# A decoder layer on one core: buffers shared by hand over three stages, even token tiles first, a written order in gate/up, right-hand tiles on 64 bytes

## The chip, the core and the metric

The kernel runs on one core of a Trainium2 chip. The metric is the device time of one execution in microseconds (us); the kernel before has a median of 1450.23 us over three runs. The engines are TensorE (PE, with its weight loads as PEld), VectorE (DVE), ScalarE (ACT), GpSimd (POOL) and SyncE (SP), which issues the transfers (DMA). PE multiplies into PSUM, in banks of 512 float32 words per partition; the other operands lie in SBUF.

## The reference

One decoder layer in float32: 1024 tokens, model width 1024, feed-forward width 2816.

```python
h  = h + rmsnorm(concat(retention, attention) @ w_o, post_mix_norm)
hn = rmsnorm(h, pre_ffn_norm)
ff = (silu(hn @ w_gate) * (hn @ w_up)) @ w_down
h  = h + rmsnorm(ff, post_ffn_norm)
h  = h + rmsnorm(p @ w_ple_proj, ple_norm) * sigmoid(h @ w_ple_gate + b_ple_gate)
```

Ahead of the first line stand a combined input projection of the normalised tokens, retention in four heads and causal attention with latents in eight heads.

## The kernel before

**Arithmetic.** Each float32 operand is split into a high and a low part (`split`: an ACT copy that rounds, L81, and a subtract, L82, on DVE unless `sub` says otherwise). A product takes three matmuls, high by high, high by low, low by high (`products`, L94, or written out). The large multiplications of gate/up and down work on 2 x 2 blocks with seven products in place of eight. For that the operands are combined by sums and differences: on the token side T1 to T4 out of the blocks of an even and an odd token tile, on the weight side the `sums`.

**Stages and lines.** (1) Input projection and latents. (2) Retention, about 162 to 291 us. Inside its loop, `down_sums(q)` is called for the 11 quarters q of w_down: it loads the four blocks of `w_down[q]` in two transfers, makes four combinations on POOL (`combos`, L108 to L111) and stores them to `td[q]` in DRAM in three transfers; the down stage loads them from there. (3) Attention. (4) The projection by w_o, about 570 to 675 us. `project(t)` runs over the token tiles 0 to 7 in order. It loads `mt` (attention output, from DRAM `mo`), `mix` and `ht`, splits `mt`, does 24 matmuls into `po`, adds (L718), takes a Square with its sum on ACT into a scrap tile `junk`, scales (L722), adds the residual (L723), takes a second Square (L726), and scales again (L728) into `mix`. `rsqrt` (L117, L119) is one DVE and one POOL operation. `operands(t)` follows two tiles behind: for an even tile it transposes B11 and B21 into the operands `xh` and `xl`; for an odd tile it makes T1 to T4 on POOL (L108 to L111) from the odd tile and the even one ahead of it, and transposes those and B22. (5) Gate/up, about 690 to 1120 us. (6) Down, from about 1140 us: seven runs of `down` over the 11 quarters, in chunks of two, each chunk with one left-hand and one right-hand slot (`dslot`: a load into `draw`, of which there are five, and a split into `dring`, nine pairs). (7) The per-layer embedding gate (`pg`) and the output.

**Gate/up.** There are 22 matrices: w_gate and w_up in 11 quarters. Each has seven products, and a product is 12 matmuls (L813) of 128 x 128 by 128 x 512. All seven of one matrix write one PSUM tile `gu` of two 512-word halves, `bank[m][0]` and `bank[m][1]`, in turn:

```python
ORDER = ((B11, 0, 0, 0), (B21, 1, 0, 1), (T2, 0, 1, 0), (T1, 1, 1, 1), (T3, 0, 2, 0), (B22, 1, 3, 0), (T4, 0, 2, 1))
```

The columns are the token operand, the half of `gu`, the weight part and its place in the part. After each product its half is evicted: for n = 0, 2 and 3 by an ACT copy (L821), for n = 1, 4 and 5 by a DVE add onto such a copy (L826), which keeps accumulating in the half, for n = 6 directly. Evicted blocks go through `use` (L797 and beside it): Silu on ACT for w_gate, a multiplication on DVE for w_up, into `ga`. Two `gu` tiles exist at a time. `weight_part` splits one part of a matrix, three steps ahead of its product; `weight_sums` makes the combinations on POOL (L776 and beside it); `load` fetches a matrix of 1 MB. `down_operands(q)` combines `ga` on POOL into `dsums` and stores both to `ld[q]`.

`steps` lists the 154 products: (0, 0), (0, 1), (1, 0), (1, 1), the rest of matrix 0, the rest of matrix 1, and then matrix by matrix. The program text emits them in that order. The order in which each engine issues is another: the tile context is opened with a timeline planner, which takes ready instructions by its own cost estimate.

**Waits.** They are drawn from the emitted order by the tile that an instruction reads or writes. In the compiled program of before, the first matmul of a product in one half of `gu` carries a wait for the eviction of the product ahead of it in the other half, where both belong to one matrix.

**Addresses.** Pools lie on the left or the right side of SBUF. Every tile on the right begins 32 bytes past a multiple of 64; the left-hand tiles that PE reads begin on a multiple. `xh`, `xl` are on the left, the weight parts `gh`, `gl` on the right; in the down stage `draw` and `dring` are both on the right.

Of the kernel before, what the change touches and what calls it, by code (L numbers as in the profile page):

```python
# [20 lines left out]
P = 128  # L21
# [41 lines left out]
def hybrid_layer(ctx: ExitStack, tc: tile.TileContext, a: dict, out: bass.AP):  # L63
# [43 lines left out]
    def combos(t1, t2, t3, t4, b11, b12, b21, b22, eng):  # L107
        eng.tensor_tensor(out=t1, in0=b12, in1=b11, op=ALU.subtract)  # L108
        eng.tensor_tensor(out=t2, in0=b22, in1=t1, op=ALU.subtract)
        eng.tensor_tensor(out=t3, in0=b22, in1=b12, op=ALU.subtract)  # L110
        eng.tensor_tensor(out=t4, in0=b21, in1=t2, op=ALU.subtract)  # L111

# [12 lines left out]

    pack = const.tile([P, sum(PACK.values())], F32, name="pack")
# [21 lines left out]
    td = [dram.tile([4, P, 512], F32, name=f"td{q}") for q in range(NQ)]  # L148
# [258 lines left out]

    def down_sums(q):
        r1, r2, s = [raws.tile([P, S], F32, tag="raw", name=n) for n in ("wd1", "wd2", "wds")]
        sp.dma_start(out=r1, in_=a["w_down"][q][:, 0:2, :].rearrange("p i n -> p (i n)"))  # L410
        sp.dma_start(out=r2, in_=a["w_down"][q][:, 2:4, :].rearrange("p i n -> p (i n)"))
        c0, c1 = slice(0, 512), slice(512, S)
        combos(s[:, c0], s[:, c1], r1[:, c1], r2[:, c0], r1[:, c0], r1[:, c1], r2[:, c0], r2[:, c1], pool)
        sp.dma_start(out=td[q][0:2].rearrange("i p n -> p i n"), in_=s.rearrange("p (i n) -> p i n", i=2))
        sp.dma_start(out=td[q][2], in_=r1[:, c1])
        sp.dma_start(out=td[q][3], in_=r2[:, c0])

    down_q = 0
    g_ret = [1.0 - 2.0 ** (-5.0 - h) for h in range(RH)]
    pending = None  # L420
    for j in range(RH // 2):
# [14 lines left out]
        for hh in range(2):  # L436
# [9 lines left out]
            for hf in range(2):  # L446
# [236 lines left out]
    B11, B21, B22, T1, T2, T3, T4 = range(7)  # L683
    st_x = ExitStack()
    px = scoped(st_x, "px")
    xh, xl = [px.tile([P, 7, 4, HALF], F32R, name=n) for n in ("xh", "xl")]
    st3 = ExitStack()
    p3 = scoped(st3, "p3", 2)
    wpm = bcast(p3, a["w_post"], "wpm")
    wpf = bcast(p3, a["w_pref"], "wpf")  # L690
# [3 lines left out]
    def to_operand(i, j, src):  # L694
        nonlocal nblk
        pt = ps1("ptx", "tfto"[nblk % 4])
# [4 lines left out]
        split(xh[:, i, :, js], xl[:, i, :, js], pt.rearrange("p (k n) -> p k n", k=4))  # L701

    tiles = {}
    lo_, hi_ = slice(0, HALF), slice(HALF, D)

    def project(t):
        mt = p3.tile([P, 4, P], F32, name="mt")
        sp.dma_start(out=mt, in_=mo[t])
        mix, ht = [p3.tile([P, D], F32, name=n, bufs=4) for n in ("mix", "ht")]
        sp.dma_start(out=mix, in_=od[t])  # L710
        sp.dma_start(out=ht, in_=a["x"][t * P : (t + 1) * P])
        mh, ml = [p3.tile([P, 4, P], F32R, name=n) for n in ("mh", "ml")]
        split(mh, ml, mt)
# [6 lines left out]
        act.activation(p3.tile([P, D], BF16, name="junk", bufs=1), mix, AF.Square, accum_out=ss)  # L720
# [5 lines left out]
        act.activation(p3.tile([P, D], BF16, name="junk", bufs=1), ht, AF.Square, accum_out=ss)  # L726
        rsqrt(ss, ss, 1.0 / D)
        dve.scalar_tensor_tensor(out=mix, in0=ht, scalar=ss, in1=wpf, op0=ALU.mult, op1=ALU.mult)  # L728
        tiles[t] = (mix, ht)

    def operands(t):
        j = t // 2
        mix, ht = tiles[t]
        if t % 2 == 0:
            to_operand(B11, j, mix[:, lo_])
            to_operand(B21, j, mix[:, hi_])
        else:
            e, he = tiles[t - 1]
            combos(he[:, lo_], he[:, hi_], ht[:, lo_], ht[:, hi_], e[:, lo_], mix[:, lo_], e[:, hi_], mix[:, hi_], pool)
            to_operand(B22, j, mix[:, hi_])  # L740
            for i, src in ((T2, he[:, hi_]), (T1, he[:, lo_]), (T3, ht[:, lo_]), (T4, ht[:, hi_])):
                to_operand(i, j, src)

    for t in range(NT):
        project(t)
        if t >= 2:
            operands(t - 2)
    st_b.close()
    operands(NT - 2)
    operands(NT - 1)  # L750
    st3.close()
# [5 lines left out]
    graw = scoped(st_g, "graw", 2, side="right")  # L757
    gsl = scoped(st_g, "gsl", 4, side="right")
    gs = scoped(st_g, "gs", 3)
    gev = scoped(st_g, "gev", 1)  # L760
    gga = scoped(st_g, "gga", 2)

    mats = [(name, q) for q in range(NQ) for name in ("w_gate", "w_up")]
    raw, sums, parts, bank, part_sums, act_out = {}, {}, {}, {}, {}, {}

    def load(m):
        name, q = mats[m]
        raw[m] = graw.tile([P, 4, HALF], F32, tag="w", name=f"raw_{name}")
        sp.dma_start(out=raw[m], in_=a[name][q])

    def weight_sums(m):
        r = raw[m]
        s = sums[m] = gs.tile([P, 3, HALF], F32, tag="s", name="sums")
        pool.tensor_tensor(out=s[:, 1], in0=r[:, 2], in1=r[:, 3], op=ALU.add)
        pool.tensor_tensor(out=s[:, 0], in0=s[:, 1], in1=r[:, 0], op=ALU.subtract)
        pool.tensor_tensor(out=r[:, 2], in0=r[:, 0], in1=r[:, 2], op=ALU.subtract)  # L776
        pool.tensor_tensor(out=s[:, 2], in0=r[:, 1], in1=s[:, 0], op=ALU.subtract)

    def weight_part(m, p):
        src = (raw[m][:, 0:2], sums[m][:, 0:2] if p == 1 else None, raw[m][:, 2:4], sums[m][:, 2:3] if p == 3 else None)[p]  # L780
        n = src.shape[1]
        hi, lo = [gsl.tile([P, 2, HALF], F32R, tag=h, name=f"{h}_{mats[m][0]}")[:, :n] for h in ("gh", "gl")]
# [8 lines left out]
    def use(m, b, v):  # L791
        name, q = mats[m]
        dst = act_out[q][:, KEPT[b]]
# [5 lines left out]
    def product(m, n):  # L799
        name, q = mats[m]  # L800
        i, b, p, at = ORDER[n]
        if n == 0:
            pt = ps2("gu")
            bank[m] = pt[:, :HALF], pt[:, HALF:]
            if name == "w_gate":
                act_out[q] = gga.tile([P, 4, HALF], F32, name="ga")
        dst = bank[m][b]
        hi, lo = parts[m, p]
        x = 0
        for k in range(4):  # L810
            ks = slice(k * P, (k + 1) * P)
            for l, r in ((hi, xh), (hi, xl), (lo, xh)):
                pe.matmul(dst, l[:, at, ks], r[:, i, k, :], start=(n in (0, 1, 3) and x == 0), stop=(x == 11),  # L813
                          skip_group_check=True)
                x += 1

        s = part_sums.setdefault(m, {})
        if n in (0, 2, 3):
            nm = {0: "s1", 2: "u2", 3: "s5"}[n]
            s[nm] = gev.tile([P, HALF], F32, name=nm, bufs=(2 if n == 0 else 1))  # L820
# [3 lines left out]
        else:  # L824
            nm, blk = {1: ("s1", 0), 4: ("s5", 3), 5: ("u2", 1)}[n]
            dve.tensor_tensor(out=s[nm], in0=dst, in1=s[nm], op=ALU.add)  # L826
            use(m, blk, s[nm])

    def down_operands(q):
        ga = act_out[q]  # L830
        s = gs.tile([P, 3, HALF], F32, tag="s", name="dsums")
# [4 lines left out]
        sp.dma_start(out=ld[q][0:4].rearrange("i p n -> p i n"), in_=ga)  # L836
        sp.dma_start(out=ld[q][4:7].rearrange("i p n -> p i n"), in_=s)
# [7 lines left out]
    def when(i, rank, f, *args):  # L845
        todo[max(i, 0)].append((rank, f, args))

    for m in range(nmat):
        first = {0: at_step[m, 0], 1: at_step[m, 2], 2: at_step[m, 4], 3: at_step[m, 5]}
        for p, i in first.items():  # L850
            when(i - 3, 2, weight_part, m, p)
# [33 lines left out]
    def td_quad(i):  # L885
        return lambda q: td[q][i]
# [164 lines left out]
```

## Time and profile before

| what | value |
|---|---|
| median of three runs | 1450.23 us (1449.12 to 1450.68) |
| the profiled execution, its own time | 1453.09 us |
| its span, first to last instruction | 1451.3 us |
| PE busy | 1361.4 us, 94% of the span, 6732 matmuls and transposes |
| DVE / ACT / POOL busy | 767.4 (53%) / 538.5 (37%) / 427.2 us (29%) |
| mean granted clock of PE | 0.976 |
| DMA | 214.73 MB, 148 GB/s on the mean, queue 1 busy for 44.2% of 16 engines' span |
| largest line of the chain that ended last | PE `gu` L813, 30% of the span |

The profile is one execution, recorded by the hardware. Busy time is a sum over instructions, less their overlap; the granted clock is the share of full speed (2.4 GHz) that PE was given, 0.5 being the lower level of 1.2 GHz. Matmuls overlap in the pipeline: a row shows 0.40 us for one of 512 columns, while the next begins 0.23 us after it. A bracket behind a row gives the idle time of the engine ahead of it and the instruction whose end released it. The chain of waits follows the last instruction back, at each step to what released it.

### The profile page before, as it was taken

Reading aid. Unit: us, or ns where it says so; the run is one execution under the profiler, and the core shown is the slowest. Engines: PE = TensorE matmul, PEld = TensorE weight load, DVE = VectorE, ACT = ScalarE, POOL = GpSimd, SP = SyncE. Lnnn points to the kernel's source line nnn. Section 1 sums busy time; section 2 is a strip of 40 time slices with the busy share of each in tenths; the row PEclk is TensorE's granted clock in tenths of the full one; section 3 lists DMA queues with packets and bytes.
Section 4 is the critical chain, followed back from the end, with each engine's and each line's share of the span. In section 5 each row is a group of like instructions: output and inputs, shape, how many; then the busy total and the mean of one; then the engine's idle time right before and its main releaser. Section 6 shows DMA issues by size and latency. Waiting matters only on the chain.

```text
span 1451.3 us, 18194 instructions
## 1 busy us (share of the span) xinstructions
PE 1361.4 (94%) x6732; PEld 1134.0 (78%) x6732; DVE 767.4 (53%) x1198; ACT 538.5 (37%) x889; POOL 427.2 (29%) x333
## 2 busy tenths in 40 slices
PE   7999999999989998876899999999997999999998
PEld 6987988788768886655688888888885788888776
DVE  6456447526577675586344444434443554474653
ACT  5343221111565554344233333333332544444421
POOL 1100344400354243237144444444443000013300
PEclk9999999999999999986999999999999999999999
DMA  6137776812565641661123332232312966575422
GB/s 242 44 123 247 264 266 232 284 52 59 163 202 145 177 113 45 226 236 50 38 109 110 109 109 92 98 109 87 109 58 98 330 203 204 187 239 181 132 72 73
DMA packets 91320, 214.73 MB, mean 148 GB/s; under 512 B 9504, under 2 KB 24096, under 8 KB 88416
## 3 DMA queue, kind: packets, MB, share of 16 engines
q1 hardware_dynamic: 91232, 213.58, 44.2%
q8 instruction: 53, 0.87, 0.3%
q14 instruction: 35, 0.29, 0.1%
HBM read 144.86 MB, written 67.63 MB: 146 GB/s over the span
## 4 chain that ended last, share of the span: by engine, by line
PE 70%; DMA 8%; DVE 7%; issue 5%; POOL 5%; ACT 3%; SPq 1%; DVEq 0%; POOLq 0%; ACTq 0%
PE gu L813 30%; PE da L902 6%; PE pg L94 5%; PE fill L94 4%; PE pa L94 4%; PE db L902 3%; PE sc L94 3%; DMA wd<-in_w_down 2%; PE prg L94 2%; PE ptp L650 2%; PE prv L94 2%; PE pge L94 2%; PE pqk L94 1%; PE po L94 1%; DMA td<-wd 1%
## 5 line engine op out<-in xcount | busy, mean ns | idle before, releaser
L813 PE MATMUL gu<-xh,gh_w_gate 128*128 128x512 f32 x308 | 123.0, 399 | 5.1 <-ACT gh_w_gate L81 1.6
L813 PE MATMUL gu<-xh,gh_w_up 128*128 128x512 f32 x308 | 122.4, 398 | 2.3 <-DVE s L826 0.9
L813 PE MATMUL gu<-xh,gl_w_up 128*128 128x512 f32 x308 | 121.9, 396 | 1.6 <-DVE gl_w_up L82 1.6
L813 PE MATMUL gu<-xl,gh_w_gate 128*128 128x512 f32 x308 | 122.5, 398 | 0.0
L813 PE MATMUL gu<-xh,gl_w_gate 128*128 128x512 f32 x308 | 122.3, 397 | 0.0
L813 PE MATMUL gu<-xl,gh_w_up 128*128 128x512 f32 x308 | 122.0, 396 | 0.0
L119 POOL TENSOR_TENSOR s<-s,mhalf 128x1 f32<-128x1 f32 x32 | 28.6, 901 | 310.3 <-DVE s L117 310.2
L641 POOL TENSOR_TENSOR pr<-pr,ri 128x128 f32<-128x128 f32 (+3 forms) x64 | 73.8, 1164 | 109.3 <-DVE ri L640 97.3
L82 DVE TENSOR_TENSOR dl_r<-raw_r,dh_r 128x1024 fp32r<-128x1024 f32 (+1 forms) x42 | 47.7, 1135 | 81.9 <-ACT dh_r L81 70.4
L832 POOL TENSOR_TENSOR dsums<-ga 128x512 f32<-128x512 f32 x11 | 14.2, 1289 | 250.4 <-DVE ga L797 250.4
L826 DVE TENSOR_TENSOR s<-gu,s 128x512 f32<-128x512 f32 x44 | 30.4, 691 | 102.0 <-PE gu L813 102.0
L81 ACT CAST dh_r<-raw_r 128x1024 fp32r<-128x1024 f32 (+1 forms) x42 | 41.3, 982 | 105.9 <-PE da L902 52.4
L902 PE MATMUL db<-dh_r,dh_l 128*128 128x512 f32 x176 | 68.1, 397 | 8.3 <-ACT dh_r L81 8.3
L813 PEld LDWEIGHTS gu<-xh,gh_w_gate 128*128 128x128 f32 x308 | 58.3, 189 | 20.6 <-ACT gh_w_gate L81 2.0
L813 PEld LDWEIGHTS gu<-xh,gh_w_up 128*128 128x128 f32 x308 | 57.9, 188 | 17.8 <-DVE s L826 1.3
L813 PEld LDWEIGHTS gu<-xh,gl_w_up 128*128 128x128 f32 x308 | 57.9, 188 | 16.0 <-DVE gl_w_up L82 2.1
L902 PE MATMUL db<-dl_r,dh_l 128*128 128x512 f32 x176 | 69.3, 394 | 0.1
L813 PEld LDWEIGHTS gu<-xh,gl_w_gate 128*128 128x128 f32 x308 | 58.2, 189 | 14.3 <-DVE gl_w_gate L82 0.2
L902 PE MATMUL db<-dh_r,dl_l 128*128 128x512 f32 x176 | 69.3, 394 | 0.0
L813 PEld LDWEIGHTS gu<-xl,gh_w_gate 128*128 128x128 f32 x308 | 58.3, 189 | 14.0
L813 PEld LDWEIGHTS gu<-xl,gh_w_up 128*128 128x128 f32 x308 | 58.0, 188 | 13.9
L82 DVE TENSOR_TENSOR tl<-ptp,th 128x512 fp32r<-128x512 f32 (+1 forms) x80 | 49.7, 633 | 24.0 <-ACT th L81 22.8
(337 smaller groups left out, 3807.2 us busy)
## 6 DMA issues: line engine op xcount, KB each, us to landing
raw_l<-ld SPq DMA_DIRECT2D x77, 256.0 KB, 3.3
wd<-in_w_down SPq DMA_DIRECT2D x22, 512.0 KB, 4.7
raw_w_gate<-in_w_gate SPq DMA_DIRECT2D x11, 1024.0 KB, 4.8
raw_w_up<-in_w_up SPq DMA_DIRECT2D x11, 1024.0 KB, 4.8
ld<-ga SPq DMA_DIRECT2D x11, 1024.0 KB, 4.3
raw_r<-td SPq DMA_DIRECT2D x44, 256.0 KB, 4.0
ld<-dsums SPq DMA_DIRECT2D x11, 768.0 KB, 3.6
raw_r<-in_w_down SPq DMA_DIRECT2D x33, 256.0 KB, 4.6
```

Of the source, the lines that this page charges most:

```text
L81: act.copy(out=hi, in_=src)
L82: sub.tensor_tensor(out=lo, in0=src, in1=hi.bitcast(F32), op=ALU.subtract)
L94: pe.matmul(dst, l, r, start=(m == 0), stop=(m == n - 1))
L119: pool.tensor_tensor(out=dst, in0=dst, in1=mhalf[:, :n], op=ALU.pow)
L641: pool.tensor_tensor(out=pr_[:, :n], in0=pr_[:, :n], in1=ri.broadcast_to([P, n]), op=ALU.mult)
L650: pe.transpose(pt[:, m * P : (m + 1) * P], pb[qq][:, kk * P : (kk + 1) * P], ident)
L813: pe.matmul(dst, l[:, at, ks], r[:, i, k, :], start=(n in (0, 1, 3) and x == 0), stop=(x == 11), skip_group_check=True)
L826: dve.tensor_tensor(out=s[nm], in0=dst, in1=s[nm], op=ALU.add)
L832: pool.tensor_tensor(out=s[:, 1], in0=ga[:, 2], in1=ga[:, 3], op=ALU.add)
L902: pe.matmul(banks[j], l[:, ls], r[:, rs_], start=(fresh and q == 0 and m == 0), stop=(q == NQ - 1 and m == 2), skip_group_check=True)
```

## The change

Buffers. Right-hand tiles get a 32-byte pad ahead of them. From the projection to the end, most tiles that were drawn from pools become fixed views of five 8 KB `duo` tiles and a 12 KB `strip`: `blk[0..9]` are halves of `duo`s; they hold `mix` and `ht` in the projection, and the accumulators and two of the five `draw` buffers in the down stage. In gate/up the same `duo`s hold one of two raw weight buffers, `gga` (the old `ga`), the evicted parts, and `quad[4]`, which is at once `wd` (the w_down quarter) and, in its first three fourths, `gs[2]` (the old `dsums`). `mt` and `junk` of a tile share bytes, two sets in turn. `xh`/`xl` become 14 tiles, one per operand and part.

Projection. Tiles run in the order 0, 2, 4, 6, 1, 3, 5, 7. The split of `mt` subtracts on POOL. The second scaling (L728) becomes a DVE multiplication by `wpf` and an ACT copy with the scale. The combinations T1 to T4 are unchanged in number, in other buffers. The loads and splits for the first products stand ahead of `operands` of the last two tiles, the first two products between these, the next two behind them.

Gate/up. `product` and `evict` are split; `steps` is unchanged. From the fifth product on, everything is emitted inside `tc.manual_schedule()`, in which each engine issues as written. w_down's combinations (`wd_load`, `wd_sums`, `wd_store`) move here out of retention: per quarter one load of 1 MB, four POOL operations, one store of 1 MB.

Down. The first chunk's slots are emitted ahead of the last `down_sums` and `down_store`.

```diff
-    def combos(t1, t2, t3, t4, b11, b12, b21, b22, eng):
...
+    pad = ctx.enter_context(tc.tile_pool(name="pad", bufs=1, side="right"))
+    pad.tile([P, 8], F32, name="pad")
...
-    def down_sums(q):
-        r1, r2, s = [raws.tile([P, S], F32, tag="raw", name=n) for n in ("wd1", "wd2", "wds")]
...
-                for _ in range(1 + (hf and h > 0)):
-                    if down_q < NQ:
-                        down_sums(down_q)
-                        down_q += 1
...
+    duo = [pst.tile([P, 2 * D], F32, name=f"duo{i}") for i in range(5)]
+    blk = [duo[i][:, j * D : (j + 1) * D] for i, j in
+           ((3, 1), (0, 1), (2, 0), (3, 0), (0, 0), (1, 0), (2, 1), (4, 0), (4, 1), (1, 1))]
+    strip = pst.tile([P, 3 * D], F32, name="strip")
...
+    order = [0, 2, 4, 6, 1, 3, 5, 7]
+
+    def project(n):
+        t = order[n]
+        v = strip[:, 2 * D + n % 2 * HALF :][:, :HALF]
+        mt, junk = v.rearrange("p (k n) -> p k n", k=4), v.bitcast(BF16)
+        mh, ml = [pmo.tile([P, 4, P], F32R, name=n_) for n_ in ("mh", "ml")]
+        mix, ht = blk[n % 7], blk[7 + n % 3]
...
-        split(mh, ml, mt)
+        split(mh, ml, mt, sub=pool)
...
-        dve.scalar_tensor_tensor(out=mix, in0=ht, scalar=ss, in1=wpf, op0=ALU.mult, op1=ALU.mult)
+        dve.tensor_tensor(out=mix, in0=ht, in1=wpf, op=ALU.mult)
+        act.activation(mix, mix, AF.Copy, scale=ss)
...
+    graw = [pg_.tile([P, 4, HALF], F32, name="graw"), quad[0]]
+    gga = [quad[2], quad[3]]
+    gs = [v.rearrange("p (i n) -> p i n", i=3) for v in (strip[:, : 3 * HALF], strip[:, 3 * HALF :])] + [quad[4][:, :3]]
+    wd = quad[4]
...
+    def wd_load(q):
+        sp.dma_start(out=wd, in_=a["w_down"][q])
+
+    def wd_sums(q):
+        b11, b12, b21, b22 = [wd[:, i] for i in range(4)]
+        pool.tensor_tensor(out=b11, in0=b12, in1=b11, op=ALU.subtract)
...
+    def wd_store(q):
+        sp.dma_start(out=td[q], in_=wd)
...
+    load(0)
+    load(1)
+    weight_part(0, 0)
+    weight_part(1, 0)
+    operands(NT - 2)
+    for m, n in steps[:2]:
+        product(m, n)
+    operands(NT - 1)
+    for m, n in steps[2:4]:
+        product(m, n)
+    for m in range(2):
+        weight_sums(m)
+    for m, n in steps[:4]:
+        evict(m, n)
+    weight_part(0, 1)
+    weight_part(0, 2)
+
+    for q in range(NQ):
+        i = 14 * q
+        if q:
+            when(i + 1, down_sums, q - 1)
+        when(max(i + 2, 4), (lambda m: weight_sums(m)) if q else (lambda m: None), 2 * q + 1)
+        if q:
+            when(i + 3, down_store, q - 1)
+        when(i + 6, wd_load, q)
+        if q + 1 < NQ:
+            when(i + 9, weight_sums, 2 * q + 2)
+        when(i + 11, wd_sums, q)
+        when(i + 13, wd_store, q)
     for m in range(nmat):
+        for p, n in enumerate((0, 2, 4, 5)):
+            if m > 1 and p == 0 or m > 0 and p or p == 3:
+                when(max(at_step[m, n] - 3, 4), weight_part, m, p)
+        if m + 2 < nmat:
+            when(at_step[m, 4], load, m + 2)
+    with tc.manual_schedule():
+        for i, (m, n) in enumerate(steps):
+            if i < 4:
+                continue
+            for f, args in todo[i]:
+                f(*args)
+            product(m, n)
+            evict(m, n)
...
+    draw = [pd_.tile([P, D], F32, name=f"draw{i}") for i in range(3)][::-1] + blk[7:9]
+    acc = blk[:7] + blk[9:]
...
+    early_slots = [down_slots(0, wd_quad(0), 0)]
+    down_sums(NQ - 1)
+    down_store(NQ - 1)
```

`product` is as before up to its last matmul, and `evict(m, n)` is what followed there. `weight_sums` has its last two lines exchanged. The remaining edits rename views.

## Rows read from the trace of the kernel before

**Rows 1.** Windows: us, five engines' busy (x), granted clock, DMA share, GB/s.

```profile
162.00:291.00 129.00, 123.56 (x743) 108.41 (x742) 72.73 (x128) 21.97 (x32) 62.17 (x48) 0.99 0.76 261
...
639.00:676.50 37.50, 16.00 (x69) 11.40 (x67) 28.16 (x37) 16.58 (x30) 20.25 (x19) 0.56 0.42 154
...
710.00:1107.00 397.00, 397.00 (x1702) 319.63 (x1703) 167.10 (x181) 134.26 (x183) 169.31 (x116) 1.00 0.26 94
```

**Rows 2.** Timeline of PE, mid gate/up: start us, us, operation.

```profile
712.87 0.40 PE L813 MATMUL gu<-xh,gh_w_up 128*128 128x512 f32 x1
...
715.67 0.40 PE L813 MATMUL gu<-xh,gh_w_gate 128*128 128x512 f32 x1
```

**Rows 3.** Timeline, ends of gate/up; bracketed: idle before, releaser.

```profile
695.00 0.50 PE L813 MATMUL gu<-xh,gl_w_up 128*128 128x512 f32 x1 [1.62 <-DVE gl_w_up L82]
...
701.84 0.50 PE L813 MATMUL gu<-xh,gh_w_gate 128*128 128x512 f32 x1 [1.44 <-ACT s L821]
...
706.13 0.49 PE L813 MATMUL gu<-xh,gh_w_gate 128*128 128x512 f32 x1 [1.22 <-DVE s L826]
...
1104.87 0.40 PE L813 MATMUL gu<-xh,gh_w_up 128*128 128x512 f32 x1
...
1107.87 0.59 ACT L821 COPY s<-gu 128x512 f32<-128x512 f32 x1 [2.20 <-PE gu L813]
...
1108.51 0.50 PE L813 MATMUL gu<-xh,gh_w_up 128*128 128x512 f32 x1 [0.68 <-ACT s L821]
...
1112.43 0.49 PE L813 MATMUL gu<-xh,gh_w_up 128*128 128x512 f32 x1 [0.85 <-DVE s L826]
```

**Rows 4.** Chain of waits: start us, us, what, x instructions.

```profile
137.19 8.20 PE pq L94 x36
...
709.97 397.88 PE gu L813 x1704
...
1160.51 29.92 PE da L902 x132
...
1410.37 33.85 PE pg L94 x144
```

**Rows 5.** Timeline of DVE, ACT, POOL and PE at the projection's end.

```profile
592.56 1.23 DVE L718 TENSOR_TENSOR mix<-po,mix 128x1024 f32<-128x1024 f32 x1 [3.67 <-PE po L94]
...
599.42 0.19 ACT L726 ACTIVATION_READ_ACCUMULATOR junk<-ht 128x1 f32 x1
...
666.78 1.28 DVE L728 SCALAR_TENSOR_TENSOR mix<-ht,s,wpf 128x1024 f32<-128x1024 f32 x1 [0.66 <-POOL s L119]
...
672.10 1.27 POOL L111 TENSOR_TENSOR ht<-mix,ht 128x512 f32<-128x512 f32 x1
...
677.31 1.05 ACT L81 CAST gh_w_gate<-sums 128x1024 fp32r<-128x1024 f32 x1
...
681.46 2.27 POOL L776 TENSOR_TENSOR raw_w_up<-raw_w_up 128x512 f32<-128x512 f32 x1
...
689.95 0.40 PE L813 MATMUL gu<-xh,gh_w_gate 128*128 128x512 f32 x1
```

**Rows 6.** Timeline of PE and chain of waits at the seam to the down stage.

```profile
1118.94 0.40 PE L813 MATMUL gu<-xh,gl_w_up 128*128 128x512 f32 x1
...
1123.19 6.94 DMA ld<-dsums
...
1130.56 9.08 DMA raw_r<-in_w_down
...
1140.81 1.19 PE L902 MATMUL db<-dh_r,dh_l 128*128 128x512 f32 x4 [0.29 <-ACT dh_r L81]
```

**Rows 7.** DMA issues: count, KB each, us to landing.

```profile
ld<-dsums SPq DMA_DIRECT2D x11, 768.0 KB, 3.6
...
raw_r<-in_w_down SPq DMA_DIRECT2D x33, 256.0 KB, 4.6
...
mt<-mo SPq DMA_DIRECT2D x8, 256.0 KB, 4.3
```

More of the change, by code (lines that the diff above doesn't have):

```diff
@@ L147, in hybrid_layer @@
     ld = [dram.tile([7, P, 512], F32, name=f"ld{q}") for q in range(NQ)]
-    td = [dram.tile([4, P, 512], F32, name=f"td{q}") for q in range(NQ)]
+    td = [dram.tile([P, 4, 512], F32, name=f"td{q}") for q in range(NQ)]
     st1 = ExitStack()
@@ L719, in project @@
         ss = small.tile([P, 1], F32, name="s3")
-        act.activation(p3.tile([P, D], BF16, name="junk", bufs=1), mix, AF.Square, accum_out=ss)
+        act.activation(junk, mix, AF.Square, accum_out=ss)
         rsqrt(ss, ss, 1.0 / D)
@@ L725, in project, with operands @@
         ss = small.tile([P, 1], F32, name="s3")
-        act.activation(p3.tile([P, D], BF16, name="junk", bufs=1), ht, AF.Square, accum_out=ss)
+        act.activation(junk, ht, AF.Square, accum_out=ss)
         rsqrt(ss, ss, 1.0 / D)
-        dve.scalar_tensor_tensor(out=mix, in0=ht, scalar=ss, in1=wpf, op0=ALU.mult, op1=ALU.mult)
[L729 to L734, printed above, removed]
+        dve.tensor_tensor(out=mix, in0=ht, in1=wpf, op=ALU.mult)
+        act.activation(mix, mix, AF.Copy, scale=ss)
+    def operands(n):
+        j = n % 4
+        mix = blk[n % 7]
+        if n < 4:
             to_operand(B11, j, mix[:, lo_])
@@ L737, in operands @@
         else:
[L738 to L741, printed above, removed]
-                to_operand(i, j, src)
[L744 to L747, printed above, removed]
+            e, ht = blk[j], blk[7 + n % 3]
+            t1, t2, t3, t4 = e[:, lo_], ht[:, lo_], mix[:, lo_], e[:, hi_]
@@ new lines, in operands @@
+            b11, b12, b21, b22 = e[:, lo_], mix[:, lo_], e[:, hi_], mix[:, hi_]
+            pool.tensor_tensor(out=t1, in0=b12, in1=b11, op=ALU.subtract)
+            pool.tensor_tensor(out=t2, in0=b22, in1=t1, op=ALU.subtract)
+            pool.tensor_tensor(out=t3, in0=b22, in1=b12, op=ALU.subtract)
+            pool.tensor_tensor(out=t4, in0=b21, in1=t2, op=ALU.subtract)
+            for i, src in ((B22, b22), (T1, t1), (T2, t2), (T3, t3), (T4, t4)):
+                to_operand(i, j, src)
+    for n in range(NT):
+        project(n)
+        if n >= 2:
+            operands(n - 2)
@@ L748, in hybrid_layer @@
+    st_m.close()
     st_b.close()
-    operands(NT - 2)
-    operands(NT - 1)
-    st3.close()
     st_g = ExitStack()
[L757 to L761, printed above, removed]
+    pg_ = scoped(st_g, "pg", side="right")
+    ghl = [[pg_.tile([P, 2, HALF], F32R, name=f"g{n}{i}") for n in "hl"] for i in range(4)]
+    quad = [v.rearrange("p (i n) -> p i n", i=4) for v in duo]
@@ L812, in product, with evict @@
             for l, r in ((hi, xh), (hi, xl), (lo, xh)):
-                pe.matmul(dst, l[:, at, ks], r[:, i, k, :], start=(n in (0, 1, 3) and x == 0), stop=(x == 11),
+                pe.matmul(dst, l[:, at, ks], r[:, k, :], start=(n in (0, 1, 3) and x == 0), stop=(x == 11),
                           skip_group_check=True)
                 x += 1
+    def evict(m, n):
+        dst = bank[m][ORDER[n][1]]
         s = part_sums.setdefault(m, {})
@@ L824, in product, with down_sums @@
         else:
-            nm, blk = {1: ("s1", 0), 4: ("s5", 3), 5: ("u2", 1)}[n]
+            nm, b = {1: ("s1", 0), 4: ("s5", 3), 5: ("u2", 1)}[n]
             dve.tensor_tensor(out=s[nm], in0=dst, in1=s[nm], op=ALU.add)
[L827 to L831, printed above, removed]
+            use(m, b, s[nm])
+    def down_sums(q):
+        ga, s = gga[q % 2], gs[2]
         pool.tensor_tensor(out=s[:, 1], in0=ga[:, 2], in1=ga[:, 3], op=ALU.add)
@@ L872, in dslot, with draw_next @@
+    junk = pd_.tile([P, D], BF16, name="junk")
+    draw = [pd_.tile([P, D], F32, name=f"draw{i}") for i in range(3)][::-1] + blk[7:9]
+    acc = blk[:7] + blk[9:]
+    wpo, wpl, bg = [strip[:, i * D : (i + 1) * D] for i in range(3)]
+    nraw = nring = 0
+    def draw_next():
+        nonlocal nraw
+        nraw += 1
+        return draw[(nraw - 1) % 5]
     def dslot(srcs, name, sub=dve):
+        nonlocal nring
         n = len(srcs)
-        raw = draw.tile([P, D], F32, tag="raw", name=f"raw_{name}")
+        raw = draw_next()
```

140 lines of the change are left out of this document (60 added, 80 removed).

## Prediction

> **What bounds the kernel now.** I read the busy times by stage first, then the chain of waits for the time of one matmul, then the timeline of TensorE (PE) at the seams between stages. PE is busy nearly all of the span, so a change pays only where PE waits, runs at the low clock, or takes longer per matmul than it must. By stage [rows 1] PE is full in gate/up (397.0 of 397.0 us), and it loses time at the end of the projection: from 639 to 676.5 it is busy for 16.0 of 37.5 us at a mean granted clock of 0.56. The retention stretch 162 to 291 loses 5.4 us. Between the last gate/up matmul and the steady run of the down stage lie another 21 us [rows 6].
>
> The timeline of gate/up holds what decides this change. In mid-stage PE alternates between two matrices: a product of w_up starts at 712.87, one of w_gate at 715.67, 2.80 us later [rows 2]. Where products of one matrix follow each other, PE stops ahead of each: at 701.84 and 1108.51 until a ScalarE copy is done, at 706.13 and 1112.43 until a VectorE add is [rows 3]. The copy that ends at 1108.46 reads one half of `gu`; the product that starts at 1108.51 writes the other half. The program's waits are those of the whole PSUM tile: product n of a matrix waits until product n-1 has been evicted, though the two use different halves. The old order hid this because the planner put a product of another matrix between them.
>
> **The change, part by part.**
>
> *The fixed order.* `steps` is unchanged: from its fifteenth entry on it runs through one matrix after the other, and before that through matrices 0 and 1. Inside the manual region every engine issues as written, so PE now gets product n, then n+1 of the same matrix, with an eviction emitted between. Products that meet the wait: matrices 0 and 1 have four each (n = 3 to 6; their n = 2 follows an eviction that is long done), the other 20 have six each (n = 1 to 6), together 128 of the 150 products of the region. Price of one, from starts of successive products: 1108.51 to 1112.43 is 3.92, 701.84 to 706.13 is 4.29, 706.13 to 709.97 is 3.84 [rows 3, 4]; an unhindered product takes 397.88 x 12 / 1704 = 2.80 [rows 4]. The excess is 1.04 to 1.49; for the ACT copy, 1104.87 to 1108.51, it is 0.84 plus 0.10 for a longer first matmul, 0.94. Three of six evictions are ACT copies, three DVE adds, two of these behind a weight split in DVE's queue. I take 1.1, with 0.94 and 1.3 as ends: 128 x 1.1 = **+141** (120 to 166). Six such stalls (7) and the wait at 695.00 (1.6) are paid today: **-8.6**. Behind a waiting eviction stand the next splits on ACT and DVE, due three products later, so they are not late; behind the waiting product stands all of PE.
>
> *The pad.* In the old program every right-hand tile begins 32 bytes past a multiple of 64, and every left-hand tile that PE reads begins on one; the pad puts the right-hand ones on multiples too. Time per 512-column matmul [rows 4]: both operands left, 8.20 / 36 = 0.228; both right, 29.92 / 132 = 0.227; one on either side, 0.2335 (gate/up) and 0.235 (`pg`). So the mixture costs, not the offset alone. All 1848 gate/up matmuls are mixed: 1848 x 0.0058 = **-10.7** (0 to -12.6). The 384 of `pg`, 192 of `po` and 288 retention matmuls on right-hand tiles are worth 864 x 0.006 = 5, of which I take **-3.5**, as `po` is paced by other engines. The Trainium skill, "SBUF — State Buffer", section "SBUF: two separate sides", says that TensorE has ports of its own and waits for nobody there, by which the place of an operand should not matter. This trace disagrees, 0.227 against 0.2335. By the page both terms would be zero and the sum 14 us higher.
>
> *Even tiles first, products beside the projection's end.* The first four products need only even tiles, yet today they start after all transposes, and the fifth starts at 689.95 [rows 5]. What the fifth needs is ready earlier: tile 7's scaling ends at 668.06, the four POOL combinations at 673.37, and the cast of the weight sums runs from 677.31 to 678.36. With the four products moved into the idle time before, the fifth can start at 678.4: **-11.5**. This holds if the chain of tile 7 keeps its time. Against it: `mt` now shares its bytes with `junk`, so the load for tile n+2 waits for the second Square of tile n. That ends 7.1 us after its last matmul (592.5 to 599.6 for tile 0), the load takes 4.3 [rows 7], the cast 0.7 with its waits, the products 24 x 0.2335 = 5.6: 17.7 us for two tiles. So the last `po` ends at 592.5 + 3 x 17.7 + 5.6 = 651 instead of 639. From there an unhindered chain is 7.1, about 2 for the power and the ACT scaling that replaces DVE's, 5.1 for four combinations, 2.5 for two sums, 1.3 for the cast: 669. With today's 39 us between last `po` and that cast it would be 690. I keep 678.4, near the middle, with 0 and -21 as ends. The split's subtract, moved to POOL, is 8 x 1.3 there for 8 x 0.7 on DVE, beside `po`.
>
> *w_down's combinations, from retention to gate/up.* Taken away: 44 POOL operations, 22 loads and 33 stores, beside 5.4 us of idle PE; **-4** (0 to -7, the idle time and the hundredth of clock). Added per q in gate/up: four POOL operations, a 1 MB load and a 1 MB store. POOL had 116 operations in 169.3 us there, 1.46 each [rows 1]; 16 per 14 products are 23 us in at least 39, nothing on the path. At the slowest rate seen, 2.27 [rows 5], they would be 36: still hidden. On SP the two `ld` stores stand ahead of the next weight load, and `wd_load` waits for them; from a load to its use there are five products, 14 us, against 3.6 to 4.6 for such a transfer [rows 7], with DMA at 0.26.
>
> *The seam to the down stage.* From the last gate/up matmul, 1119.3, to 1140.8 PE does 48 matmuls worth 10.9 us [rows 6], so 10.6 are lost. Now the first chunk is loaded ahead, but the second chunk's right operand goes to `blk[7]`, whose bytes hold `dsums` until their store has landed: 3.9 from the last product to that store, 3.6 to 6.9 for it, 4.6 to 9.1 for the load, 1.3 for the cast, together 13.4 to 21, less 5.4 for the first chunk: 8 to 16 lost [rows 6, 7]. I take **+2** (-3 to +5). The down stage itself keeps its 0.227.
>
> **Sum.** 141 - 8.6 - 10.7 - 3.5 - 11.5 - 4 + 2 = +104.7. The profiled execution took 1453.1 us (span 1451.3 and 1.8 around it), 2.9 above the median of the runs, 1450.2. So 1557.8 by the profile, **1555** by the median.
>
> **Rivals.**
>
> *A product waits only for its own half.* The eviction of n-1 then runs beside product n, and the 141 us vanish: 1555 - 141 = **1414**, faster than before. For it: the halves are different banks of 512 words, and nothing in the arithmetic asks for the wait. Against it: all six sequences of this kind in the trace stop, each until the other half has been evicted. It decides once the stall falls below 105 / 128 = 0.8 us. 0.14. The Trainium skill, "PSUM — Partial Sum Buffer", section "PSUM bank collisions raise a hardware error", says that two engines on different banks run clean side by side; here the trace shows that only across tiles, with one matrix evicted beside the other's product [rows 2].
>
> *The pitch stays 0.2335*, because the two sides differ by more than the offset: 1555 + 14 = **1569**. For it: left and right also lie apart. Against it: gate/up and `pg` show the same excess at quite different distances. 0.15. This is what the SBUF page's rule would make of the pad.
>
> *Evictions queue behind casts*, as ahead of 701.84, where the idle time alone was 1.44: 1.7 us each is 218 instead of 141, **1632**. Against it: the written order puts no cast ahead of the copies of n = 0 and n = 3. 0.05.
>
> **How the numbers follow.** Forecast as summed 0.62; pitch unchanged 0.15; own half only 0.14; queueing 0.05; something between, with part of the stalls hidden, 0.04. The forecast's own spread is the stall's 120 to 166 with the first seam's ends: 1525 to 1590. To hold 8 in 10 the range takes in the unchanged pitch and stops short of the faster case: 1505 to 1600. A difference under 0.2% can't be told from none here. Slower: 0.62 + 0.15 + 0.05 + 0.03 = 0.85; same 0.01; faster 0.14.
>
> **What would show it.** In the profile after: PE stopping 0.7 to 0.9 us ahead of six of seven gate/up products, ended by ACT copies and DVE adds, so that it is busy for some three quarters of the stage; 12 matmuls of a product in 2.73 us; the fifth product near 674; no POOL combinations between 162 and 291; PE idle for 8 us or more after the down stage's first 24 matmuls. The prediction is wrong if successive products of one matrix start 2.7 us apart.

## The result, and the profile after

The changed kernel takes **1571.99 us** (median of four runs, 1570.62 to 1575.86), the kernel before beside it 1450.45: a ratio of 1.0844, 95% interval 1.0823 to 1.0864. It is slower, by 121.5 us. Predicted were 1555, 1505 to 1600. The profiled execution after took 1571.66 us, its span is 1569.9, that of before 1451.3: the 118.6 us between the spans are what is laid out here.

The windows of the profile after (columns as in [rows 1]):

```profile
162.00:291.00 129.00, 129.00 (x835) 117.42 (x834) 65.36 (x124) 24.62 (x39) 4.03 (x4) 1.00 0.30 95
...
640.00:692.00 52.00, 38.24 (x168) 30.03 (x168) 38.10 (x41) 24.40 (x41) 42.54 (x31) 0.83 0.28 96
692.00:1100.00 408.00, 337.88 (x1356) 247.81 (x1356) 136.94 (x144) 103.39 (x147) 197.29 (x130) 1.00 0.36 124
```

PE no longer waits in retention, and it is busy for 83% of gate/up, where it had been full. The granted clock there stays at 1.00, the level of 2.4 GHz: some 0.7 us of idle time at each product did not lower it. The view of waits of after, for PE (what it waited for, us in total, times, longest), names the cause:

```profile
PE gu L807 <- DVE duo L823: 50.2, 64, 0.9
PE gu L807 <- ACT duo L818: 43.6, 64, 1.0
```

These are 128 stops, the number that the prediction counted, half behind ACT copies and half behind DVE adds. The chain of waits shows four products in mid-stage (start us, us, what):

```profile
790.62 3.03 PE gu L807 x12
...
793.67 0.59 ACT duo L818
...
794.31 3.03 PE gu L807 x12
...
797.36 0.70 DVE duo L823
...
798.11 3.04 PE gu L807 x12
...
801.18 0.70 DVE duo L823
...
801.92 5.76 PE gu L807 x24
```

The chain goes to and fro between PE and the eviction: a product, to the end of its last matmul, 3.03; the copy 0.59; the next product. From start to start it is 3.69 behind a copy and 3.81 behind an add. Only the 24 matmuls at 801.92 run through: the last product of one matrix and the first of the next, in another `gu`. In [rows 2] such a pair was the rule.

Where the 118.6 us lie, from the starts of the matmuls that bound the stages:

| stretch | before | after | difference | forecast |
|---|---|---|---|---|
| start to the first attention score | 357.75 | 346.56 | -11.2 | -4 and part of the pad |
| to the last attention and fill product | 224.94 | 223.59 | -1.3 | 0 |
| to the fifth gate/up product | 107.26 | 121.44 | **+14.2** | -11.5 and part of the pad |
| to the last gate/up matmul | 428.99 | 543.23 | **+114.2** | +121.7 (141 - 8.6 - 10.7) |
| to the last matmul of `db` | 224.76 | 226.25 | +1.5 | +2 |
| to the end | 107.6 | 108.8 | +1.2 | part of the pad |

The +14.2 falls in three. From the last `fill` product (`fill` is what PE does between the products of attention) to the first `po` matmul of the projection it takes 9.90 us, before 2.09; from there to the last `po` 77.11, before 53.89; on to the fifth product 34.43, before 51.28: +7.8, +23.2 and -16.8. The second and third are looked at below. The first stands in the timelines of SP and PE, of before and then of after:

```profile
578.21 0.36 SPq L708 DMA_DIRECT2D mt<-mo  x1
...
583.84 0.32 SPq L575 DMA_DIRECT2D od<-fill  x1
...
584.79 0.50 PE L94 MATMUL po<-bh,mh 128*128 128x512 f32 x1 [1.70 <-ACT mh L81]
```

```profile
571.29 0.33 SPq L555 DMA_DIRECT2D od<-fill  x1
...
572.97 0.45 SPq L700 DMA_DIRECT2D strip<-mo  x1
...
580.05 0.79 PE L94 MATMUL po<-bh,mh 128*128 128x512 f32 x1 [9.51 <-ACT mh L81]
```

Before, the first load of `mt` is issued 5.6 us ahead of the last store of `fill`; after, it stands behind that store in SP's queue, and PE is idle for 9.51 us. All kernels below with the whole change have a gap of 9.5 to 11.0 us here, those built on the kernel before one of 1.1 to 3.4. Which part of the change turned load and store round was not tried.

### The profile page after: what moved, and what is told of

It reads as the page before. It is cut to its first block, busy times and chain, and to the rows that moved or that the text cites. A ratio compares the mean times of both kernels' runs of the same rounds, so it can differ in the third digit from the quotient of the medians.

```text
span 1569.9 us, 18052 instructions
## 1 busy us (share of the span) xinstructions
PE 1386.1 (88%) x6732; PEld 1130.9 (72%) x6732; DVE 759.0 (48%) x1190; ACT 542.7 (35%) x897; POOL 454.3 (29%) x341
## 4 chain that ended last, share of the span: by engine, by line
PE 75%; DVE 8%; ACT 5%; issue 4%; DMA 4%; POOL 3%; SPq 0%; DVEq 0%; ACTq 0%; POOLq 0%
PE gu L807 28%; PE db L961 7%; PE pqk L94 6%; PE da L961 6%; PE pa L94 4%; PE fill L94 3%; PE prv L94 3%; DVE duo L823 3%; ACT duo L818 2%; PE sc L94 2%; PE po L94 2%; PE pg L94 2%; PE ptp L630 1%; PE prg L94 1%; PE pge L94 1%
## 5 line engine op out<-in xcount | busy, mean ns | idle before, releaser
L807 PE MATMUL gu<-xh,gh 128*128 128x512 f32 x616 | 257.2, 417 | 98.7 <-DVE duo L823 50.2
L807 PE MATMUL gu<-xh,gl 128*128 128x512 f32 x616 | 242.9, 394 | 0.0
L807 PE MATMUL gu<-xl,gh 128*128 128x512 f32 x616 | 242.9, 394 | 0.0
L807 PEld LDWEIGHTS gu<-xh,gh 128*128 128x128 f32 x616 | 116.5, 189 | 173.4 <-DVE duo L823 77.2
L807 PEld LDWEIGHTS gu<-xh,gl 128*128 128x128 f32 x616 | 116.8, 190 | 26.4
L807 PEld LDWEIGHTS gu<-xl,gh 128*128 128x128 f32 x616 | 116.8, 190 | 21.1
L113 POOL TENSOR_TENSOR s<-s,mhalf 128x1 f32<-128x1 f32 x32 | 24.0, 753 | 276.1 <-DVE s L111 276.1
L82 DVE TENSOR_TENSOR gl<-duo,gh 128x1024 fp32r<-128x1024 f32 x22 | 34.8, 1583 | 108.8 <-ACT gh L81 108.8
L113 POOL TENSOR_TENSOR gf<-gf,mhalf 128x4 f32<-128x4 f32 x8 | 8.1, 1008 | 266.6 <-DVE gf L111 266.6
L82 DVE TENSOR_TENSOR dl<-draw,dh 128x1024 fp32r<-128x1024 f32 (+1 forms) x52 | 59.2, 1155 | 49.8 <-ACT dh L81 49.7
L961 PE MATMUL db<-dl,dh 128*128 128x512 f32 x176 | 69.9, 397 | 4.1 <-DVE dl L82 4.1
L961 PE MATMUL db<-dh,dh 128*128 128x512 f32 x176 | 68.9, 399 | 4.9 <-ACT dh L81 4.9
L961 PE MATMUL db<-dh,dl 128*128 128x512 f32 x176 | 69.7, 396 | 0.0
```

Source lines behind the costliest of these rows:

```text
L82: sub.tensor_tensor(out=lo, in0=src, in1=hi.bitcast(F32), op=ALU.subtract)
L113: pool.tensor_tensor(out=dst, in0=dst, in1=mhalf[:, :n], op=ALU.pow)
L807: pe.matmul(dst, l[:, at, ks], r[:, k, :], start=(n in (0, 1, 3) and x == 0), stop=(x == 11), skip_group_check=True)
L961: pe.matmul(banks[j], l[:, ls], r[:, rs_], start=(fresh and q == 0 and m == 0), stop=(q == NQ - 1 and m == 2), skip_group_check=True)
```

## The experiments

The interval behind each ratio is of 95%; each ratio is to the kernel before, run on the same chip.

### Two PSUM tiles for the two halves

```diff
-            pt = ps2("gu")
-            bank[m] = pt[:, :HALF], pt[:, HALF:]
+            bank[m] = [ps1("gu", g) for g in ("tt", "fo")[m % 2]]
...
-    operands(NT - 2)
+    operands(NT - 2, "s")
```

> The kernel after, with the two halves of each gu as two PSUM tiles of one bank each (and the transposes of the last two token tiles in the banks that gu had). Theory: the stalls come from a wait of the whole tile. In the profile after, products 12 matmuls long follow each other after 3.70 to 3.81 us where one would take 2.73, at 128 places. Then these go and the time is 1572 - 128 x 1.03 = 1440, 1432 to 1450, with gate/up some 411 us long. Rival: the written order is slow by itself, because evictions and weight splits come late in their queues or the buffers shared by hand wait for each other; then stalls of the same kind move to weight splits or copies and the time stays above 1500.

Measured: 1441.4 us, 0.9947 (0.993 to 0.9965). One edit of the tiles, with the order as written, takes 131 us off and brings the kernel 0.5% below the one before. (The transposes of the last two token tiles go to the banks that `gu` had; that is the second half of the edit.) The chain of waits of this run:

```profile
693.41 405.48 PE gu L807 x1787
```

Gate/up is one piece, 405.48 / 1787 = 0.2269 us a matmul, and no wait of a product for an eviction is left. From the fifth product to the last matmul it takes 409.4 us against 543.2: 133.8 for 128 stops, **1.05 us each**. While PE writes one bank, ACT and DVE read the other, and PE keeps its pace. The Trainium skill ("PSUM — Partial Sum Buffer", section "PSUM bank collisions raise a hardware error") says that engines on different banks run clean side by side; this run agrees, and that the pace holds is what it adds, 0.2269.

### The planner in place of the written order

```diff
-    with tc.manual_schedule():
+    with ExitStack():
```

> The kernel after, with the manual region taken away, so that the planner orders gate/up; tiles and buffers stay. Theory: the wait of the whole tile stays, but products of two matrices come in turn again and cover it, as before: only stalls at the ends are left (8 to 15 us), 1440 to 1455. Rival: the shared buffers themselves hold the products back, then the planner can't help and it stays above 1500.

Measured: 1488.0 us, 1.0268 (1.024 to 1.0297), between the theory and its rival. Products of two matrices alternate again, and of the 128 stops 31 are left (34 us). But they have a new reason. The timeline of SP, POOL, ACT and PE:

```profile
804.89 0.33 SPq L851 DMA_DIRECT2D td<-duo  x1
805.31 0.38 SPq L764 DMA_DIRECT2D duo<-in_w_up  x1
...
812.44 1.05 ACT L81 CAST gh<-duo 128x1024 fp32r<-128x1024 f32 x1 [9.01 <-DMA duo<-in_w_up]
...
814.80 0.68 DVE L823 TENSOR_TENSOR duo<-gu,duo 128x512 f32<-128x512 f32 x1
...
815.53 0.50 PE L807 MATMUL gu<-xh,gh 128*128 128x512 f32 x1 [1.84 <-DVE duo L823]
```

and the waits of SP over the stage:

```profile
SPq L851 <- POOL duo L848: 110.2, 11, 11.7
```

The store of w_down's combinations stands in SP's queue ahead of the next load of a weight matrix, and it waits for POOL, 110 us over 11 stores (29.9 in the run with two tiles, where the load of w_up at 783.76 stands ahead of the store at 786.62). So, as I read these rows, the weights come late, ACT splits them late, the DVE subtract of that split delays the eviction behind it, and PE waits for that eviction; the order on SP was not tried by itself. The longest wait of this queue, 156.2 us of the `ld` stores for DVE, is 95.6 in the run with two tiles, where nothing stops for it. The order by hand was worth something; what spoilt it was the tile.

### w_down's combinations back in retention

```diff
+                for _ in range(1 + (hf and h > 0)):
+                    if down_q < NQ:
+                        wd_early(down_q)
...
-        when(i + 6, wd_load, q)
-        when(i + 11, wd_sums, q)
-        when(i + 13, wd_store, q)
```

> The kernel after, with the combinations of w_down back in retention (loads, four POOL operations and three stores for each quarter) and out of gate/up. The prediction gave this part 4 us; the two traces show 11 us less from 162 us to the first attention product. If that is all the combinations, 1572 + 11 = 1583 and PE waits in retention again. If most of it is the alignment of the right-hand tiles, 1576 or less. Rival for gate/up: the combinations also cost there; then that stage gets shorter by more than 2 us.

Measured: 1584.9 us, 1.0944 (1.0914 to 1.0974), 13 above the changed kernel. The first attention score starts at 356.96 again, 10.4 us later, and gate/up keeps its length from the fifth product on (543.7, with them 543.2), so there they cost nothing. Its window, and one wait of the stretch 155 to 360:

```profile
162.00:291.00 129.00, 123.74 (x742) 109.23 (x741) 72.84 (x126) 21.83 (x31) 63.62 (x48) 0.97 0.77 263
```

```profile
ACT hi_r L81 <- DMA raw_r<-in_w_rqkg: 26.6, 8, 9.3
```

So the combinations cost retention 10.4 us. Idle time (5.3) and the clock (an estimate from its mean: 3% of 129, 3.9) make 9.2 of it. That weights for q and k come late, because each quarter takes three of the four `raws` buffers, is how I read this wait, which the changed kernel does not have; it was not tried by itself.

### Without the pad, and the pad alone

```diff
-    pad = ctx.enter_context(tc.tile_pool(name="pad", bufs=1, side="right"))
-    pad.tile([P, 8], F32, name="pad")
```

> The kernel after without the 32-byte pad. Theory: a 512-column matmul whose operands lie on the two kinds of addresses takes 0.2335 us in place of 0.2275. Then a gate/up product takes 2.80 in place of 2.73, 10.7 us in all as the stalls come on top, and retention, projection and pg a further 3 to 5: 1572 + 14 = 1586. Rival: where an operand lies makes no difference, 1572 within 3 us.

Measured: 1580.96 us, 1.0916 (1.089 to 1.0942), 9 above the changed kernel. The other way round, the same two lines put into the kernel before:

> The kernel before with the 32-byte pad alone. Theory: 1848 gate/up matmuls at 0.2275 in place of 0.2335, as in the profile after (0.227) against that without the pad (0.233): -11; the 384 of pg and some of retention and the projection: -3; 1450 - 14 = 1436, 1434 to 1441. Rival: gate/up ends no earlier, as the end is set by other engines: 1448 or more.

Measured: 1436.45 us, 0.991 (0.9875 to 0.9945). The chains of waits, the changed kernel without the pad first, then the kernel before with it:

```profile
794.40 3.08 PE gu L805 x12
```

```profile
136.89 8.16 PE pq L94 x36
...
708.16 386.62 PE gu L815 x1704
...
1147.15 29.92 PE da L904 x132
```

386.62 / 1704 = 0.2269, where [rows 4] had 0.2335: the pad takes 11.6 us off gate/up there (417.4 from the fifth product, before 429.0). `pq`, with both operands on the left, moves from 0.228 to 0.227, and `da`, with both on the right, takes 29.92 us for 132 with the pad as without it [rows 4], though the pad shifts both. So it is the mixture that costs. Under the stops the pad gives less, 6.4 us from the fifth product on: twelve matmuls take 3.03 with it and 3.08 without, 0.05 in place of 0.07. So where an operand begins does matter here. The prediction set the Trainium skill ("SBUF — State Buffer", section "SBUF: two separate sides") against this, by which PE never waits on anyone at its ports. That rule speaks of waits between engines and not of where an operand begins: it gave no reason to expect a pad of no worth, and the two runs do not contradict it.

### The kernel before with two tiles, and with both

> The kernel before with the halves of gu as two PSUM tiles, nothing else. Theory: the planner's order covers nearly every wait of the whole tile, so only the seven stops at both ends of gate/up (8.6 us) can go: 1442 to 1450. Rival: a planner that is free to run ahead changes its order and loses as much elsewhere: 1450 or more.

Measured: 1441.94 us, 0.9954 (0.9935 to 0.9973). Gate/up from the fifth product on is 419.8 in place of 429.0, so its stops did cost 9.

> The kernel before with the 32-byte pad and the two PSUM tiles, nothing else of the change. Alone the pad gave 0.991 and the tiles 0.9954; they act on different times (a pitch, and stops), so together 0.984 to 0.988, 1427 to 1433 where before is 1450. If the planner loses one of the gains by another order: 0.990 or more.

Measured: 1428.62 us, 0.9866 (0.985 to 0.9883). The gains add up.

### A scrap of its own

From here on the kernel with two tiles is the base.

```diff
-        mt, junk = v.rearrange("p (k n) -> p k n", k=4), v.bitcast(BF16)
+        mt, junk = v.rearrange("p (k n) -> p k n", k=4), xs[6][0][:, :, 2 * P :]
```

> The kernel of the two tiles (1441), in which the scrap of the Squares no longer shares its bytes with mt (it goes to a part of an operand tile that is written only later). Theory: the pace of the projection, 20.6, 18.6 and 22.2 us for two token tiles, comes from mt's load, which waits for the second Square of two tiles before. Without that the last po matmul ends some 15 us earlier (656 to about 641). The end of the time follows only as far as POOL lets it: between the last po and the fifth gate/up product POOL works without a pause for 27 us (four combinations, eight weight sums, four combinations). If the chain just moves ahead, 1441 - 15 = 1426; if POOL's weight sums, which wait for nothing in the projection, then fill the gain only in part, 1426 to 1436. Rival: the projection's pace is set by the subtract on POOL or by ACT, then 1438 or more.

Measured: 1432.01 us, 0.9885 (0.9859 to 0.991). In the kernel after, the timelines of ACT, SP and POOL show the wait (a Square, mt's load for two tiles on, its split):

```profile
594.85 1.06 ACT L716 ACTIVATE strip<-duo 128x1024 bf16<-128x1024 f32 x1 [3.50 <-DVE duo L713]
...
596.06 0.32 SPq L700 DMA_DIRECT2D strip<-mo  x1
...
598.95 0.62 ACT L81 CAST mh<-strip 128x512 fp32r<-128x512 f32 x1
...
599.70 2.26 POOL L82 TENSOR_TENSOR ml<-strip,mh 128x512 fp32r<-128x512 f32 x1 [1.46 <-ACT mh L81]
```

The load is issued as the Square ends. The first `po` matmul that reads `ml` starts at 602.02, as the subtract on POOL ends, 20.6 us after the same matmul of two tiles before, at 581.40. With a scrap of its own the last `po` starts at 632.9 in place of 656.1, 23 us earlier; the fifth product only 11.5 earlier, at 680.3. (The attention stage ended 2.9 us earlier in this execution; counted from there it is 20 and 8.6.) The other half is lost on POOL, here in the kernel after:

```profile
668.75 2.27 POOL L733 TENSOR_TENSOR duo<-duo 128x512 f32<-128x512 f32 x1
670.99 2.26 POOL L768 TENSOR_TENSOR strip<-duo 128x512 f32<-128x512 f32 x1
...
679.14 0.55 POOL L113 TENSOR_TENSOR s<-s,mhalf 128x1 f32<-128x1 f32 x1
...
683.41 2.24 POOL L731 TENSOR_TENSOR duo<-duo 128x512 f32<-128x512 f32 x1
685.62 2.25 POOL L770 TENSOR_TENSOR strip<-graw,strip 128x512 f32<-128x512 f32 x1
...
690.73 1.73 POOL L734 TENSOR_TENSOR duo<-duo,duo 128x512 f32<-128x512 f32 x1
```

Weight sums (L768 to L771) stand ahead of the last tile's power (L113, 679.14) and between its combinations (L731 to L734). In the kernel before, the sums came behind them.

### Attempts on POOL's queue, and on the seam to the down stage

The next three runs build on the one with a scrap of its own. The subtract back on DVE, and the second matrix's sums moved into the written region:

```diff
-        split(mh, ml, mt, sub=pool)
+        split(mh, ml, mt)
...
-    for m in range(2):
-        weight_sums(m)
+    weight_sums(0)
...
+        when(max(i + 2, 4), weight_sums, 2 * q + 1)
```

> As the run before (two tiles, scrap of its own), with the subtract of mt's split back on DVE and the four weight sums of the second matrix moved from ahead of the last token combinations into the written region. Theory: POOL's queue at the end of the projection gets 5 to 8 us shorter and the fifth product starts that much earlier: 6 us below the run before, about 1420 to 1430. Rival: PE waits for transposes of the last tile whose time is set by DVE or ACT; then no difference, or slower by the eight subtracts of 0.7 us on DVE.

Measured: 1434.1 us, 0.9897 (0.9874 to 0.9921): no gain. All eight sums still ran ahead of the last combinations (680.46 to 685.53): the region orders its own instructions, and the planner still sets them against the rest. So the next run took the seam into the region:

```diff
     with tc.manual_schedule():
+        for m, n in steps[:4]:
+            product(m, n)
+        for m, n in steps[:4]:
+            evict(m, n)
+        operands(NT - 1, "s")
+        for m in range(2):
+            weight_sums(m)
+            if m == 0:
+                weight_part(0, 1)
+        weight_part(0, 2)
```

> The kernel with two tiles and a scrap of its own (1432), in which the written region begins earlier: the first four products and their evictions, the transposes and combinations of the last tile, and only then the eight weight sums. The run before had the second matrix's sums inside the region, but on POOL they still stood ahead of the last four combinations, as the region keeps its own order only. Theory: with the combinations of the last tile ahead of the sums the fifth product starts at 667 to 674 in place of 680: 1420 to 1427. Rival: the wait only changes its name, since the fifth product then needs sums that come after the combinations, or since PE, in written order, stands at a transpose of the last tile while products could run: 1430 or more.

Measured: 1429.03 us, 0.9853 (0.9827 to 0.9878). POOL and PE of this run:

```profile
670.51 1.74 POOL L735 TENSOR_TENSOR duo<-duo,duo 128x512 f32<-128x512 f32 x1
672.21 1.26 POOL L769 TENSOR_TENSOR strip<-graw 128x512 f32<-128x512 f32 x1
...
676.96 1.09 PE L689 MATMUL ptx<-pack,duo 128*128 128x128 f32 x4 [0.64 <-DVE xl L82]
679.67 0.79 PE L807 MATMUL gu<-xh,gh 128*128 128x512 f32 x1 [1.62 <-ACT gh L81]
```

The combinations now end at 672.2, 8 us earlier than with the planner's order, but the fifth product starts at 679.67, 0.65 earlier: it waits for the split of sums that now come last. As the rival had it, the wait changed its name. A part is left, though: in this execution the stage ahead ended 2.6 us later. Counted from the last `fill` product the fifth starts after 108.6 us, in place of 111.8 (and 113.4 in the next run, which differs only behind gate/up). That is the 3 us between the medians; the intervals overlap.

```diff
-        return draw[(nraw - 1) % 5]
+        return draw[(nraw - 1) % 5] if nraw not in (4, 5) else strip[:, (nraw - 4) * D : (nraw - 3) * D]
```

> The kernel with two tiles and a scrap of its own (1432), in which the fourth and fifth load of the down stage go to free bytes of the strip and not to the tile that holds the last sums until their store has landed. Theory: the second chunk's right-hand operand needn't wait for that store; the two idle times of PE behind the first chunk (6.6 and 3.3 us) and the low clock behind them go in part: from the last gate/up product to the last matmul of db 229 us become 222 to 225, so 1425 to 1428. Rival: the left-hand operands, which hang on the stores as well, or the number of transfers at once set it: 1430 or more.

Measured: 1428.1 us, 0.9854 (0.983 to 0.9878), 222.6 us from the last gate/up matmul to the last of `db` in place of 229.1. In the kernel after, the chain of waits at this seam and the timeline of PE; then PE of the run with a scrap of its own; then DVE and PE of this run:

```profile
1239.06 6.77 DMA ld<-duo
...
1246.57 3.82 DMA duo<-in_w_down
```

```profile
1240.16 0.50 PE L961 MATMUL db<-dl,dh 128*128 128x512 f32 x1 [4.05 <-DVE dl L82]
...
1251.56 2.05 PE L961 MATMUL db<-dh,dh 128*128 128x512 f32 x4 [4.92 <-ACT dh L81]
```

```profile
1095.96 0.79 PE L961 MATMUL db<-dl,dh 128*128 128x512 f32 x1 [3.28 <-DVE dl L82]
...
1109.74 2.08 PE L961 MATMUL db<-dh,dh 128*128 128x512 f32 x4 [6.64 <-ACT dh L81]
```

```profile
1094.04 4.10 DVE L82 TENSOR_TENSOR dl<-strip,dh 128x1024 fp32r<-128x1024 f32 x2
...
1101.53 0.79 PE L961 MATMUL db<-dl,dh 128*128 128x512 f32 x1 [6.62 <-DVE dl L82]
```

After, PE stops twice: 4.05 in the first chunk, for a subtract that stands on DVE behind the last eviction of gate/up, and 4.92 ahead of the second chunk, whose right-hand load waits for the store of the sums in the same bytes. With a scrap of its own the two are 3.28 and 6.64. With other bytes the second stop is gone. The first is longer, 6.62, since the second chunk's subtracts, 4.10 us, now stand on DVE ahead of the first chunk's. So stops of 9.9 us became 6.6; the rest of the 6.5 us fits the clock, whose mean over the first 55 us behind the last gate/up matmul is 0.94 in place of 0.88 (an estimate: 6% of 55, 3.3).

> Both edits of the two runs before. They touch seams 400 us apart, so their gains add up if the theories hold: 1413 to 1424; if neither holds, 1430.

Measured: **1424.61 us**, 0.9817 (0.9798 to 0.9837), the fastest of all, just above the range. Its four times (1421.27 to 1425.46) lie below all four of the run ahead, on the same chip (1426.21 to 1431.7), so the written seam is worth 3.5 us here.

## Why the prediction held, and where it did not

**The stalls.** Right in place, kind and number. The wait of the whole tile meets 128 products, and each costs 1.05 us, not 1.1: 133.8 in place of 141. The rival that a product waits for its own half alone falls with the 128 stops, and the run with two tiles shows what it would have been worth; it came to 1441 and not to 1414, mainly since the terms at the start of gate/up fell short. Its turning point was miscounted: without the stalls the sum is -36.3, so the sign turns at 36.3 / 128 = 0.28 us a stall and not at 0.8. The 1.05 lies above both.

**The old stalls and the pad in gate/up.** -8.6 and -10.7 were -9.2 and -11.6, each alone in the kernel before. Under the stops the pad gave 6.4. The rival that the pitch stays is out by the chains above.

**The pad elsewhere.** -3.5 came only in part. Without the pad the first attention score starts 2.0 us later. `pg` has 0.227 with the pad and without it, since the change put all its operands on the left; its gain of 384 x 0.006 went into more waits, and from the last `db` to the end it is 1.2 longer.

**The start of gate/up.** This step failed: -11.5 (0 to -21) was +14.2. Three of its terms were off. The projection was taken to begin when it had begun; its first `po` comes 7.8 us later, behind a store that stands ahead of the first load, and that was not seen. The wait through the shared scrap was named and priced at 17.7 us for two tiles, +12 up to the last `po`; it was 20.5, 19.6 and 18.8 from first matmul to first, and the last tile starts 12.3 behind the one ahead of it and not 5.6, +23.2 in all. The subtract on POOL, put beside `po`, stands on this path (2.26 at 599.70). Behind the last `po` I put the chain of one tile, with two sums, and took a middle value, 27 us; it was 34, of which 26 are POOL's queue with the combinations of two tiles and eight weight sums among them, which in the old order came behind the combinations. "This holds if the chain of tile 7 keeps its time" was the condition, and it did not.

**Retention.** -4 (0 to -7) was -11.2, of which undoing the combinations gives back 10.4 (undoing the pad 2.0, so the two overlap). The bound was taken from idle time and clock of one window of before, 5.4 us and 0.01 of 129; the clock of such a window came out at 0.97 in the run that undoes this part. About 1 us of its 10.4 has no row here; and in before itself idle time and clock make 6.7 (5.4 and 1.3), so the size stays in part open.

**The seam to the down stage.** +2 was +1.5, with the wait where it was put, a right-hand operand behind the store of the sums (4.92, where 8 or more were forecast), and one that was not seen, the first chunk's own subtract on DVE (4.05). Evictions queueing behind casts were not seen: no stop is longer than 1.0 us.

The errors at the seam (+25.7), in retention (-7) and in gate/up (-7.5) in part cancel; the sum, +104.7, came to +118.6.

## What to carry to other kernels

Before an order is fixed by hand, look at what the waits are drawn from: where two parts of one tile are used in turn, give them two tiles, as the order that hides a needless wait may be the one that is taken away. Buffers shared to save space turn into waits of the load that comes next, so follow each share to the engine that releases it and to what stands behind it in that queue. Of this change, two small edits of the kernel before (an aligned right side, two PSUM tiles) give 1428.62, a ratio of 0.9866: about three quarters of what the whole change gave once it was mended, 0.9817, with the late first load of `mt` still in it.

## What was not expected of the hardware

A POOL operation of 128 x 512 in float32 takes 1.27 or 2.25 us, on the same lines and in the same stretch (the rows of POOL above are of this shape, but for L113). In the trace after, from 575 to 1240 us, 52 took over 2.0 us, and DVE was busy for 71% of their time on the mean and for no less than 47%; of 135 that took up to 1.4 us it was for 27%. So the slow ones lie beside DVE's work; that DVE slows them was not tried.

Stops cost the pitch too: with a stop ahead of most products, consecutive matmuls lie 0.2297 us apart on the mean (not counting the first two of a product, 0.34), without stops 0.2267. With mixed operands this does not show: 0.2331 with stops, in the changed kernel without the pad, and 0.2333 in the kernel before. So the pad gains less under stops; why, no run here shows.
